# FFN down panels: low weight parts from an adding transfer instead of VectorE

## The chip, the cores and the metric

The kernel runs on one core of a Trainium2 chip. The metric is the device time of one execution in microseconds (us). The engines are named as the profile names them: PE is TensorE's matrix multiply and PEld its weight load, DVE is VectorE, ACT is ScalarE, POOL is GpSimd, and SP is SyncE, which here only issues transfers.

## What is computed

Two sequences of 256 tokens with 1024 features pass through a trunk of two layers. Each layer is a half-step gated feed-forward (FFN), a token mixer (a state-space mixer in the first layer, gated delta-net in the second), and a second FFN, each behind an RMS norm. Everything is float32. The change lies in the four FFNs:

```python
def swiglu(x, w_gu, w_down):
    gate, up = jnp.split(x @ w_gu, 2, axis=-1)
    return (jax.nn.silu(gate) * up) @ w_down

x = x + 0.5 * swiglu(rmsnorm(x, ffn1_norm[i]), ffn1_w_gu[i], ffn1_w_down[i])
```

`w_down` is 2816 by 1024. The 512 tokens are the columns of every tile, features lie on the 128 partitions.

## The kernel before, in words

To keep float32 accuracy at the matrix engine's rounded type (`fp32r`), every matrix is carried as a high part h (the value rounded to `fp32r`) and a low part l (the value less h). One product of a 128x128 weight block with a 128x512 tile is three matmuls, h·a, h·b and l·a, where a and b are the activations' two parts (lines 215, 216 and 217, in `multiply`).

The weights' parts are made in `halves`, a generator. Its inner generator `loads` walks over panels. A panel of `w_down` is one block of 128 output features, 22 weight blocks deep, so an FFN has 8 panels. SP loads up to 8 blocks into a raw tile `wr` (line 189; 512 KB for 8 blocks, 384 KB for 6; three buffers). Then, for each chunk of up to 4 blocks, ACT copies the raw values to the high tile `wh`, which rounds them (line 195; three buffers), and DVE subtracts `wh` from the raw values into the low tile `wl` (line 196; three buffers). A panel's 22 blocks are thus five chunks of 4 and one of 2. The wrapper `feed` traces one chunk ahead of the one in use.

`multiply` takes chunks from the feed and issues three matmuls per block into one PSUM tile named `pd`: 12 matmuls for a chunk of 4, 6 for a chunk of 2. All 22 blocks of a panel add up in the same `pd`. A buffer of `wh` is free again after the last line-216 matmul of its chunk, one of `wl` after the last line-217 matmul. With three buffers each, the parts of a chunk can be made while the two chunks before it are multiplied.

`ffn` first makes the hidden activations (gate and up products, tiles `p`, `pg`, `pu`). The down stage follows: a feed over the 8 panels, the first two of them cut into pieces of 8, 8 and 6 blocks and taken in turn, since the last hidden tiles come late, and then panels 2 to 7 one after the other. After each panel DVE adds the half step to the residual (line 343). Then, for the next stage, ACT and DVE split the new residual tile (lines 99 and 100), ACT squares it (line 106) and POOL adds the squares up (lines 108 and 110).

Instructions are placed on the engines' queues by the framework's planner in the order of a simulated timeline, with semaphores between engines. Each engine then works through its own queue in order; a waiting instruction holds up those behind it. POOL issues no transfer in the kernel before: all go through SP.

Of the kernel before, what the change touches and what calls it, by code (L numbers as in the profile page):

```python
# [13 lines left out]
F32 = mybir.dt.float32  # L14
F32R = mybir.dt.float32r
AF = mybir.ActivationFunctionType
ALU = mybir.AluOpType
# [20 lines left out]
class Trunk:  # L38
# [131 lines left out]
            parts.append(self.split(u[:], self.par[:, g + t:g + t + 1], self.xnp, "xn", f"xn{t}"))  # L170
        return parts

    def halves(self, panels, between=None):


        nc = self.nc
        def loads():
            for src in panels:
                for k1 in range(0, src.shape[1], 8):
                    m = min(8, src.shape[1] - k1)  # L180
                    raw = self.wr.tile([P, m, P], F32, tag="w", name="wr")
                    if between and src is panels[0]:

                        nc.sync.dma_start(raw[:, 0:4], src[:, 0:4, :])
                        between(0)
                        nc.sync.dma_start(raw[:, 4:8], src[:, 4:8, :])
                        between(1)
                    else:
                        nc.sync.dma_start(raw[:], src[:, k1:k1 + m, :])
                    for k0 in range(0, m, 4):  # L190
                        n = min(4, m - k0)
                        h = self.wh.tile([P, n, P], F32R, tag="w", name="wh")
                        l = self.wl.tile([P, n, P], F32R, tag="w", name="wl")
                        r = raw[:, k0:k0 + n, :]
                        nc.scalar.activation(h[:], r, AF.Copy)  # L195
                        nc.vector.tensor_tensor(l[:], r, h[:].bitcast(F32), op=ALU.subtract)  # L196
                        yield h, l, n
        def feed(ahead):
            while ahead is not None:
                now, ahead = ahead, next(g, None)  # L200
                yield now

        g = loads()
        return feed(next(g))

# [40 lines left out]
    def ffn(self, x, g, wgu, wd, load=None):  # L246
# [3 lines left out]
        nc, tc = self.nc, self.tc  # L250
        feed = self.halves([wgu[j, :, s] for j in range(NP) for s in range(2)], load)
# [3 lines left out]
        with tc.tile_pool(name="hid", bufs=10, reuse_waits="tile") as hp:  # L255
            hid = []
            with tc.tile_pool(name="form", bufs=6, reuse_waits="tile") as fp, \
                    tc.tile_pool(name="quad", bufs=3, reuse_waits="tile") as qp, \
                    tc.tile_pool(name="pgu", bufs=5, space=bass.MemoryType.PSUM, reuse_waits="tile") as pp:
                for j in range(NP):  # L260
# [9 lines left out]
                    a = self.t("t")  # L270
                    b = self.t("v")
# [4 lines left out]
                    h = hp.tile([P, 2, NT], F32R, name=f"h{j}", tag="p", bufs=NP)  # L276
# [10 lines left out]
                for q in range((NF - NP) // 2):  # L287
# [3 lines left out]
                    for n in range(7):  # L291
# [10 lines left out]
                        if n == 0:  # L302
                            a = sb("a", "t")
# [10 lines left out]
                        elif n == 4:  # L314
                            b = sb("b", "v")
# [11 lines left out]
            with tc.tile_pool(name="hhi", bufs=len(held), reuse_waits="tile") as hh:  # L327
                for v in held:
                    h, l = (pool.tile([P, 2, 2, 256], F32R, name="hh", tag="h") for pool in (hh, hp))
                    act(h[:], v[:], AF.Copy)  # L330
                    tt(l[:], v[:], f32(h[:]), op=ALU.subtract)
                    hid += [(h[:, :, e, :], l[:, :, e, :]) for e in range(2)]

                cut = (0, 8, 16, NF)
                feed = self.halves([wd[m][:, a:b, :] for a, b in zip(cut, cut[1:]) for m in range(2)] + [wd[m] for m in range(2, 8)])
                first = [self.multiply(feed, hid, "pd") for _ in range(2)]
                for a, b in zip(cut, cut[1:3]):
                    for f in first:
                        for _ in range(a, b):
                            next(f)  # L340
                for m in range(8):
                    p = self.run(first[m] if m < 2 else self.multiply(feed, hid, "pd"))
                    stt(x[m][:], p[:], -0.5, x[m][:], op0=ALU.mult, op1=ALU.add)
# [953 lines left out]
```

## Time and profile before

| what | us |
|---|---|
| median of two runs | 2579.3 |
| lowest and highest run | 2577.03 and 2581.57 |
| the profiled execution's own time | 2575.13 |
| its span, first to last instruction | 2573.3 |

The span is what the trace covers; about 2 us lie around it. In the rows, a line names the source line, the engine, the operation, the tile written and those read, then counts and times. `x192` is a count. "Idle before" is the time in which the engine had nothing to do just before such an instruction, and the arrow names what ended the wait. A busy matmul row is longer than the distance to the next one, since matmuls are pipelined; the distance between starts is the rate.

### The profile page before, as it was taken

The numbers are of one execution on the slowest core, as the hardware profiler recorded it, in microseconds if no ns is written. First come the engines' busy times: TensorE is split into PE (matmuls) and PEld (weight loads), VectorE is DVE, ScalarE is ACT, GpSimd is POOL, SyncE is SP. The second block draws the span as 40 slices with busy tenths as digits, with TensorE's granted clock in tenths as the row PEclk, the third lists the DMA queues.
The fourth block names the chain that finished last, engine by engine and source line by source line (L and its number), as shares of the span: only waits on it lengthen the run. The fifth ranks groups of instructions, "written<-read, shape, count | busy, mean of one in ns | idle before, by whom it ended". The sixth has DMA issues, their size and how long they took to land. (4 is left out here: it accounts for less than half of the span.)

```text
span 2573.3 us, 39462 instructions
## 1 busy us (share of the span) xinstructions
PE 2517.8 (98%) x15352; PEld 2207.1 (86%) x15352; DVE 1892.6 (74%) x2894; ACT 1227.8 (48%) x2178; POOL 361.8 (14%) x317
## 2 busy tenths in 40 slices
PE   8999999999999999999999999999999999999998
PEld 6999787777777899988999887888888988899976
DVE  6998438888874899735998537878787874799833
ACT  4445336666663544433444435445555554444521
POOL 1000004665743000000000002000100101000000
PEclk9999999999999999999999999999999999999999
DMA  4332332222222333233333343543434443333232
GB/s 154 105 108 80 90 97 71 73 84 71 81 78 91 120 108 102 72 96 112 114 107 89 94 121 109 148 114 108 123 111 120 122 126 113 120 107 107 72 97 78
DMA packets 192267, 263.32 MB, mean 102 GB/s; under 512 B 59984, under 2 KB 110416, under 8 KB 192080
## 3 DMA queue, kind: packets, MB, share of 16 engines
q1 hardware_dynamic: 192080, 260.81, 33.8%
q8 instruction: 120, 1.97, 0.3%
q14 instruction: 67, 0.55, 0.1%
HBM read 240.32 MB, written 20.45 MB: 101 GB/s over the span
## 5 line engine op out<-in xcount | busy, mean ns | idle before, releaser
L196 DVE TENSOR_TENSOR wl<-wr,wh 128x512 fp32r<-128x512 f32 (+1 forms) x525 | 380.7, 728 | 416.0 <-ACT wh L195 405.6
L195 ACT ACTIVATE wh<-wr 128x512 fp32r<-128x512 f32 (+1 forms) x525 | 319.5, 611 | 636.9 <-PE pd L216 321.7
L395 ACT ACTIVATE qh<-wq 128x1024 fp32r<-128x1024 f32 x144 | 153.0, 1062 | 183.2 <-PE p L300 143.6
L216 PE MATMUL pd<-hh,wh 128*128 128x512 f32 x576 | 228.9, 397 | 0.0
L217 PE MATMUL pd<-hh,wl 128*128 128x512 f32 x576 | 226.7, 395 | 1.3 <-DVE wl L196 1.3
L215 PE MATMUL pd<-hh,wh 128*128 128x512 f32 x576 | 226.6, 395 | 0.3
L395 ACT ACTIVATE qh<-s 128x1024 fp32r<-128x1024 f32 x108 | 114.8, 1063 | 179.6 <-PE p L300 171.8
L396 DVE TENSOR_TENSOR ql<-wq,qh 128x1024 fp32r<-128x1024 f32 x144 | 175.7, 1220 | 10.8 <-ACT qh L395 10.7
L396 DVE TENSOR_TENSOR ql<-s,qh 128x1024 fp32r<-128x1024 f32 x108 | 131.8, 1221 | 30.0 <-ACT qh L395 30.0
L108 POOL COPY acc<-sq 128x512 f32<-128x512 f32 x8 | 5.4, 680 | 1027.6 <-issue 999.4
L215 PEld LDWEIGHTS pd<-hh,wh 128*128 128x128 f32 x576 | 108.1, 188 | 29.2 <-ACT wh L195 2.0
L217 PEld LDWEIGHTS pd<-hh,wl 128*128 128x128 f32 x576 | 108.1, 188 | 28.5 <-DVE wl L196 3.0
L216 PEld LDWEIGHTS pd<-hh,wh 128*128 128x128 f32 x576 | 108.1, 188 | 25.5
L110 POOL TENSOR_TENSOR acc<-acc,sq 128x512 f32<-128x512 f32 x57 | 76.7, 1346 | 349.3 <-ACT sq L106 345.1
L215 PE MATMUL pz<-xn,wh 128*128 128x512 f32 x248 | 101.1, 408 | 2.9 <-ACT wh L195 2.9
L217 PE MATMUL pz<-xn,wl 128*128 128x512 f32 x248 | 101.0, 407 | 2.7 <-DVE wl L196 2.5
L216 PE MATMUL pz<-xn,wh 128*128 128x512 f32 x248 | 99.1, 400 | 0.9 <-DVE xn L100 0.8
L301 PE MATMUL p<-f1h,ql 128*128 128x256 f32 x288 | 82.3, 286 | 1.9 <-DVE ql L396 1.9
L300 PE MATMUL p<-f1l,qh 128*128 128x256 f32 x288 | 82.3, 286 | 0.0
L299 PE MATMUL p<-f1h,qh 128*128 128x256 f32 x288 | 82.2, 285 | 0.0
L299 PE MATMUL p<-f2h,qh 128*128 128x256 f32 x288 | 81.6, 283 | 0.0
L301 PE MATMUL p<-f2h,ql 128*128 128x256 f32 x288 | 81.5, 283 | 0.0
(491 smaller groups left out, 7911.6 us busy)
## 6 DMA issues: line engine op xcount, KB each, us to landing
wq<-in_f_gu SPq DMA_DIRECT2D x144, 512.0 KB
wr<-in_f_wd SPq DMA_DIRECT2D x64, 512.0 KB
wr<-in_ssd_w SPq DMA_DIRECT2D x48, 512.0 KB
wr<-in_gdn_w SPq DMA_DIRECT2D x48, 512.0 KB
wr<-in_f_gu SPq DMA_DIRECT2D x31, 512.0 KB
wr<-in_f_wd SPq DMA_DIRECT2D x32, 384.0 KB
wr<-in_ssd_out SPq DMA_DIRECT2D x12, 512.0 KB
wr<-in_gdn_out SPq DMA_DIRECT2D x11, 512.0 KB
```

The source lines that it names most:

```text
L108: nc.gpsimd.tensor_copy(acc[:], sq[:])
L110: nc.gpsimd.tensor_tensor(acc[:], acc[:], sq[:], op=ALU.add)
L195: nc.scalar.activation(h[:], r, AF.Copy)
L196: nc.vector.tensor_tensor(l[:], r, h[:].bitcast(F32), op=ALU.subtract)
L215: mm(p[:], h[:, q, :], a[:], start=k == 0, stop=False)
L216: mm(p[:], h[:, q, :], b[:], start=False, stop=False)
L217: mm(p[:], l[:, q, :], a[:], start=False, stop=k == K - 1)
L299: mm(p[:, e], h[:, e, k, :], fh[:, k, :], start=(e, k) == (0, 0), stop=False)
L300: mm(p[:, e], h[:, e, k, :], fl[:, k, :], start=False, stop=False)
L301: mm(p[:, e], l[:, e, k, :], fh[:, k, :], start=False, stop=(e, k) == (1, 3))
L395: nc.scalar.activation(h[:], v, AF.Copy)
L396: tt(l[:], v, h[:].bitcast(F32), op=ALU.subtract)
```

## The change

`halves` gets a flag `lean`, which only the down stage sets. With it, the low part is formed in two steps: ACT copies `wh` with scale -1 into `wl`, and a transfer issued by POOL reads the same weights from memory a second time and adds them to `wl` in place. The raw tile is still loaded by SP, and only ACT reads it. All other users of `halves` keep the subtract on DVE.

```diff
-    def halves(self, panels, between=None):
+    def halves(self, panels, between=None, lean=False):
...
                         nc.scalar.activation(h[:], r, AF.Copy)
-                        nc.vector.tensor_tensor(l[:], r, h[:].bitcast(F32), op=ALU.subtract)
+                        if lean:
+                            nc.scalar.activation(l[:], h[:].bitcast(F32), AF.Copy, scale=-1.0)
+                            nc.gpsimd.dma_start(l[:], src[:, k1 + k0:k1 + k0 + n, :], accum_op=ALU.add)
+                        else:
+                            nc.vector.tensor_tensor(l[:], r, h[:].bitcast(F32), op=ALU.subtract)
                         yield h, l, n
...
-                feed = self.halves([wd[m][:, a:b, :] for a, b in zip(cut, cut[1:]) for m in range(2)] + [wd[m] for m in range(2, 8)])
+                feed = self.halves([wd[m][:, a:b, :] for a, b in zip(cut, cut[1:]) for m in range(2)] + [wd[m] for m in range(2, 8)], lean=True)
```

## Rows read from the trace of the kernel before

**Rows 1.** The page: span and busy time of each engine.

```profile
span 2573.3 us, 39462 instructions
PE 2517.8 (98%) x15352; PEld 2207.1 (86%) x15352; DVE 1892.6 (74%) x2894; ACT 1227.8 (48%) x2178; POOL 361.8 (14%) x317
```

**Rows 2.** Four down stages: us; PE, PEld, DVE, ACT, POOL busy; clock, DMA share, GB/s.

```profile
262.00:374.00 112.00, 111.59 (x478) 89.17 (x477) 42.59 (x64) 35.82 (x59) 8.41 (x7) 1.00 0.32 96
1072.00:1184.00 112.00, 111.61 (x484) 89.50 (x483) 48.53 (x68) 37.90 (x61) 8.39 (x7) 1.00 0.29 86
1434.00:1546.00 112.00, 112.00 (x485) 90.23 (x484) 42.17 (x64) 35.41 (x59) 9.64 (x10) 1.00 0.42 125
2446.00:2558.00 112.00, 111.69 (x481) 89.74 (x480) 35.54 (x55) 29.69 (x49) 8.34 (x7) 1.00 0.28 82
```

**Rows 3.** Waits in the first down stage: who for whom; us, times, longest.

```profile
ACT wh L195 <- PE pd L216: 74.1, 44, 2.4
DVE wl L196 <- ACT wh L195: 63.7, 34, 2.6
...
PE pd L217 <- DVE wl L196: 0.3, 1, 0.3
```

**Rows 4.** Timeline of the matmuls, 300 to 307 us: start, length, first matmuls of chunks.

```profile
300.71 0.39 PE L215 MATMUL pd<-hh,wh 128*128 128x512 f32 x1
...
303.51 0.39 PE L215 MATMUL pd<-hh,wh 128*128 128x512 f32 x1
...
306.31 0.39 PE L215 MATMUL pd<-hh,wh 128*128 128x512 f32 x1
```

**Rows 5.** Timeline of PEld: the weight load of that last chunk's first low part.

```profile
306.55 0.19 PEld L217 LDWEIGHTS pd<-hh,wl 128*128 128x128 f32 x1
```

**Rows 6.** Timeline of ACT, 296 to 316 us.

```profile
298.84 0.73 ACT L99 ACTIVATE xn<-x,par 128x512 fp32r<-128x512 f32 x1 [0.32 <-DVE x L343]
299.47 0.62 ACT L106 ACTIVATE sq<-x 128x512 f32<-128x512 f32 x1
300.74 0.63 ACT L195 ACTIVATE wh<-wr 128x512 fp32r<-128x512 f32 x1 [0.66 <-PE pd L216]
...
306.28 0.42 ACT L195 ACTIVATE wh<-wr 128x256 fp32r<-128x256 f32 x1 [2.12 <-PE pd L216]
```

**Rows 7.** Timeline of DVE, 296 to 316 us: low parts of 4 and of 2 blocks.

```profile
301.41 0.69 DVE L196 TENSOR_TENSOR wl<-wr,wh 128x512 fp32r<-128x512 f32 x1 [1.06 <-ACT wh L195]
...
306.73 0.42 DVE L196 TENSOR_TENSOR wl<-wr,wh 128x256 fp32r<-128x256 f32 x1 [1.85 <-ACT wh L195]
```

**Rows 8.** Timeline of POOL, 262 to 400 us: sums per panel, the longest operation.

```profile
300.23 1.30 POOL L110 TENSOR_TENSOR acc<-acc,sq 128x512 f32<-128x512 f32 x1 [14.10 <-ACT sq L106]
315.63 1.30 POOL L110 TENSOR_TENSOR acc<-acc,sq 128x512 f32<-128x512 f32 x1 [14.10 <-ACT sq L106]
...
386.52 2.94 POOL L169 TENSOR_TENSOR t<-x,rstd 128x512 f32<-128x512 f32 x1 [6.40 <-DVE xn L100]
```

**Rows 9.** The chain of waits, 2085 to 2120 us: two 256 KB loads, release to landing.

```profile
2090.18 2.45 DMA ob<-opark
...
2109.86 3.22 DMA ob<-opark
```

**Rows 10.** The tile ob: SP's issue of such a load, ns min/median/max.

```profile
L992 SPq DMA_DIRECT2D ob<-opark x12: 319/319/447, 2082.9 to 2114.6; - x12
```

**Rows 11.** Groups of POOL: a small and a large one; busy us, mean ns.

```profile
L169 POOL TENSOR_TENSOR t<-x,rstd 128x512 f32<-128x512 f32 x4 | 8.4, 2112 | 12.8 <-DVE xn L100 12.8
...
L127 POOL TENSOR_TENSOR sr<-sv,mhalf 128x4 f32<-128x4 f32 x8 | 8.2, 1022 | 87.0 <-DVE sv L126 87.0
```

**Rows 12.** Transfers, 262 to 374 us: packets, MB, share of 16 engines.

```profile
q1 hardware_dynamic: 3168, 10.62, 31.9%
```

**Rows 13.** The chain of waits, 1794 to 1804 us: the slowest 256 KB transfer read.

```profile
1796.55 5.79 DMA CU<-dtt
```

**Rows 14.** A gapped stretch of the second mixer, columns as in rows 2.

```profile
1700.00:1760.00 60.00, 52.99 (x375) 48.21 (x374) 43.21 (x122) 28.36 (x80) 7.22 (x9) 0.97 0.31 83
```

## The prediction

> **What bounds the kernel now.** The page comes first. Matmuls are busy 98% of the span, DVE 74%, ACT 48%, POOL 14% [rows 1]. Only work taken off PE, or PE's idle time, can shorten the kernel. So I look at the stretches that the change touches. Inside the four down stages PE is busy at least 111.59 of 112 us at the full granted clock, while DVE stands at 36 to 49 us and ACT at 30 to 38 [rows 2]. The waits say the same from the other side: PE waited 0.3 us in all for a low part, once, while DVE waited 63.7 us for ACT, and ACT 74.1 us for PE to give a buffer back [rows 3]. So neither DVE nor ACT is late: both are held by the three buffers, and the parts lie ready long before their use. The reader should take from this that the change removes work from an engine that PE does not wait for. What decides is whether its replacement still fits into the time that three buffers give.
>
> That time is read from the timelines. Chunks of 4 blocks start at 300.71, 303.51 and 306.31, so a chunk lasts 2.80 us [rows 4], and a chunk of 2 by half the matmuls 1.40. A panel is five and a half such, 15.40, which is the distance of POOL's sums [rows 8]. The chunk at 306.31 uses the buffers of the one that ended at 300.71. Its high part was started at 300.74 for 0.63 us [rows 6], its low part at 301.41 for 0.69 [rows 7], so it was ready at 302.10. It was wanted at 306.55 [rows 5]: 4.45 us to spare.
>
> **The change part by part.**
>
> *Removed from DVE.* 4 FFNs with 8 panels give 160 subtracts of 0.69 and 32 of 0.42 us [rows 7]: 124 us of DVE, next to nothing of it waited for by PE. If all idle PE time of rows 2 came back, that is 1.1 us over the four stretches. I take 0 and keep -1.
>
> *Added to ACT.* 192 negations of the shape of line 195, 0.63 or 0.42 us [rows 6]: 114 us. Per panel ACT then does 5 x 1.26, 0.84 and the 1.35 of lines 99 and 106: 8.5 of 15.4 us. It stays off the bound as a rate. The negation waits for `wl`'s buffer, which comes one matmul after `wh`'s; queued behind it are the next line 195, 99 and 106, which are due later anyway. It costs its own length in the latency below.
>
> *Moved.* The raw tile is released by ACT instead of DVE, 0.7 us earlier; SP's next load waits for that release, with three tiles of two chunks ahead. Worth 0; it makes the next load coincide with the adding transfer of the same chunk. POOL's one sum of 1.30 us per panel [rows 8] shares its queue with six issues; a sum queued behind them is not due before the next norm, but a chunk's issue behind a sum can be late by up to 1.30.
>
> *Added: the transfer.* No row shows a transfer issued by POOL or one that adds, so I bound it. Call D the time from the end of the negation to the landing.
> - Issue: at the least what SP takes, 0.32 [rows 10]; POOL's small two-input operation takes 1.02, a large one 2.11 on the mean [rows 11]. I take 1.02, because an issue touches little data.
> - Movement and landing: a plain 256 KB load took 2.45 to 3.22 us with SP's issue of 0.32 inside [rows 9, 10], and the slowest 256 KB transfer read took 5.79 [rows 13]. I take 3.22 less 0.32, 2.90, because every adding transfer runs beside the panels' loads.
> - The add: the destination must be read too. At worst this costs as much engine time as moving the bytes once. In the first stretch 10.62 MB took 31.9% of 16 engines over 112 us [rows 12], that is 35.7 us, so 0.262 MB takes 0.88. At best it overlaps and costs 0. I take 0.88.
>
> D = 1.02 + 2.90 + 0.88 = 4.80 us. The ends are 2.45 (issue as SP's, free add) and 1.02 + 5.47 + 0.88 = 7.37; with an issue of 2.11 as well, 8.46.
>
> The 256 KB row can be weighed against a rule. The Trainium skill ("DMA: Bandwidth & Descriptors", Anatomy of one DMA) gives a POOL-issued transfer about 2.0 us plus its bytes at 436 GB/s, so 2.6 by estimate, and in Latency and other measured facts about 1 us to the first byte; as an estimate D would be 3.6, which is the hidden case below. Rows 9 agree for SP's transfers; no run here shows POOL's. The rule that speaks against the change is in "Collectives: The Full Stack" (The bandwidth ceiling): an adding transfer reads two sources over one queue and moves half as fast. That would make the estimate 4.2, and the cost +28 us.
>
> **The sum.** After a chunk ends, its buffer's next low part is negated 1.33 us later (300.71 to 301.37 for the high part, 0.04 hand-over as in rows 6 and 7, 0.63 for the negation: 302.04), with 0.04 to reach POOL: 1.37. PE wants the part 0.24 after a chunk's start [rows 4, 5]. So the next chunk in that buffer can't start before 1.13 + D after the last one ended. Each buffer serves two chunks per panel. The buffers that hold two chunks of 4 come round in 2 x 2.80 + 2 x (1.13 + D) = 7.86 + 2D. A panel needs 15.40, so the break-even is D = 3.77, and beyond it a panel lengthens by 2 us for each us of D. With 32 panels:
>
> cost = 64 x (D - 3.77) = 64 x 1.03 = +66 us.
>
> The profiled execution took 2575.1, which is 4.2 below the median of the runs; on it the sum gives **2641 us**, +2.6%. A 60 us stretch with PE busy 88% was granted 0.97 of the clock [rows 14]; the lap above leaves PE 88% busy as well, which would add at most 3% of the 5.6 us of matmul in a lap, 0.17 x 32 = 5 us. I leave that in the range.
>
> **The rivals.**
> - *Hidden.* D stays below 3.77: POOL issues in about a third of a microsecond, or landing is the 2.45 of the quiet row and the add is free (2.45 + 0.70 = 3.15 with POOL's issue). Then the panel's own 15.40 covers it, and time stays at 2574 to 2576. For it: 4.45 us of slack in a full chunk. Against it: the short chunk takes 1.40 of that from two chunks per panel (3.05 is left), and the pair of half panels at a stage's start has two short chunks close together. This is the side "not slower"; it decides at D = 3.77 for no cost, and at D = 4.57 for less than 51 us.
> - *The transfer is much slower*, because adding bytes move slower than copied ones, or the queues fill: raw loads already use 0.28 to 0.42 of the transfer engines [rows 2], and the added ones read as many bytes again from memory and from `wl`. At 7.37 the cost is 64 x 3.60 = +230: 2805 us. Against it: the quiet rows of the same size stay at or under 3.22.
> - *POOL's queue is the bound.* Six issues per panel of 2.11 and a sum of 1.30 take 14.0 us, under 15.4; only from 2.35 us per issue would the queue itself set the pace. At the 2.94 of POOL's longest operation [rows 8] per issue, six and a sum take 18.9, and 32 panels lose 3.5 each: +114, 2689 us. It would show as POOL going from issue to issue without a wait.
> - *Faster.* The planner orders all queues by its own timeline, and with other orders elsewhere the time may move; DVE's 124 us lie where PE does not wait. To gain 2% PE would have to lose idle time of 51 us, and the whole span holds 2573.3 - 2517.8 = 55.5 [rows 1], 1.1 of it in these stretches. 3%.
>
> **How the numbers follow.** I give the exposed landing (D from 3.8 to 6.2) 0.60, hidden 0.20, slower transfer or POOL-bound 0.17, another order that gains 0.03. About 2%, 51 us, is what a measurement of this kernel can tell from no change; that is D = 4.57. Of the 0.60 I put 0.48 above that and 0.12 below; with the 0.17 slower gets 0.65, same 0.20 + 0.12 = 0.32, faster 0.03. The likeliest case alone runs from 2577 to 2731 (D = 6.2). The range takes in the hidden case and most of the slow one: 2573 to 2780, which is D = 6.97.
>
> **What would show it.** Right: in the down stages PE waits for `wl` at line 217, two or three times a panel, and the panel's distance at POOL's sums goes from 15.40 to about 17.5; DVE's busy time falls by about 124 us and ACT's rises by 114; bytes read rise by 46 MB (192 chunks, 4 x 11.5). The wait of ACT for `pd` stays, that of DVE for `wh` is gone there. The waits should fall on the first two chunks after a short one. Wrong: if PE stays at 111.6 of 112, D is below 3.77 and the transfer is cheaper than rows 9 and 11 say; if all chunks are late alike, D is far above 5 or POOL's issues are the bound; if the lost time lies outside the four stretches, the planner's order has changed and the lap is not the cause.

## The result and the profile after

The changed kernel took 2686.63 us (median of two runs, 2685.92 to 2687.34) against 2579.3: slower, ratio 1.0436 with a 95% interval of 1.042 to 1.0453. Its span is 2685.5 us, 112.2 longer. The page of the kernel after, its parts on engines and queues (compare [rows 1]):

```profile
span 2685.5 us, 39810 instructions
PE 2540.4 (95%) x15352; PEld 2203.6 (82%) x15352; DVE 1774.6 (66%) x2702; ACT 1331.9 (50%) x2370; POOL 531.2 (20%) x509
...
q1 hardware_dynamic: 192080, 260.81, 32.2%
q0 software_dynamic: 27648, 46.15, 11.5%
...
L198 POOL DMA_DIRECT2D wl<-in_f_wd x192 | 168.0, 884 | 1267.3 <-ACT wl L197 649.3
...
L221 PE MATMUL pd<-hh,wl 128*128 128x512 f32 x576 | 236.8, 413 | 64.7 <-DMA wl<-in_f_wd 64.1
```

DVE lost 118 us of work and ACT gained 104, near the 124 and 114 forecast, and 46.15 MB come on a new queue. The last line is the price: the matmul of the low part, which had waited next to never [rows 3], now sits idle 64.7 us before its groups on `hh` alone, and what it waits for is the adding transfer. The line numbers have moved by 4: 217 is 221 here.

Panels are best measured by DVE's residual update, one per panel. Its timeline in the second down stage of the kernel after:

```profile
1133.85 0.69 DVE L347 SCALAR_TENSOR_TENSOR x<-pd,x 128x512 f32<-128x512 f32 x1 [3.87 <-PE pd L221]
1152.71 0.69 DVE L347 SCALAR_TENSOR_TENSOR x<-pd,x 128x512 f32<-128x512 f32 x1 [16.40 <-PE pd L221]
1170.64 0.69 DVE L347 SCALAR_TENSOR_TENSOR x<-pd,x 128x512 f32<-128x512 f32 x1 [15.48 <-PE pd L221]
1188.46 0.69 DVE L347 SCALAR_TENSOR_TENSOR x<-pd,x 128x512 f32<-128x512 f32 x1 [15.36 <-PE pd L221]
```

Between these the distance is 17.8 to 18.9 us where it was 15.40 [rows 8]. Taken over all panels by the same rows, the six later panels of a stage lost 17.6, 19.0, 26.7 and 16.9 us in the four stages, 80.2 in all; the stretch from the previous stage's end to the end of the second panel lost 5.1, 8.9, 8.9 and 9.1, 32.0 in all. Together that is the 112.2. The second kind of stretch also holds the mixers and the gate and up stages; that its loss arises at the starts of the down stages is shown by the experiment on them below.

How a late part arises is seen in one round of the buffers. The timeline of POOL in the kernel after, then the weight loads that waited for a transfer:

```profile
1149.97 0.86 POOL L198 DMA_DIRECT2D wl<-in_f_wd  x1 [2.37 <-ACT wl L197]
1152.77 0.89 POOL L198 DMA_DIRECT2D wl<-in_f_wd  x1 [1.94 <-ACT wl L197]
1154.17 0.87 POOL L198 DMA_DIRECT2D wl<-in_f_wd  x1 [0.51 <-ACT wl L197]
1155.05 1.31 POOL L110 TENSOR_TENSOR acc<-acc,sq 128x512 f32<-128x512 f32 x1
1158.24 0.88 POOL L198 DMA_DIRECT2D wl<-in_f_wd  x1 [1.88 <-DMA wl<-in_f_wd]
1162.22 0.86 POOL L198 DMA_DIRECT2D wl<-in_f_wd  x1 [3.10 <-ACT wl L197]
1164.58 0.88 POOL L198 DMA_DIRECT2D wl<-in_f_wd  x1 [1.50 <-ACT wl L197]
1167.89 0.87 POOL L198 DMA_DIRECT2D wl<-in_f_wd  x1 [2.42 <-ACT wl L197]
```

```profile
1154.14 0.19 PEld L221 LDWEIGHTS pd<-h,wl 128*128 128x128 f32 x1 [1.44 <-DMA wl<-in_f_wd]
1158.10 0.19 PEld L221 LDWEIGHTS pd<-hh,wl 128*128 128x128 f32 x1 [1.33 <-DMA wl<-in_f_wd]
1163.79 0.19 PEld L221 LDWEIGHTS pd<-hh,wl 128*128 128x128 f32 x1 [0.25 <-DMA wl<-in_f_wd]
1166.60 0.19 PEld L221 LDWEIGHTS pd<-hh,wl 128*128 128x128 f32 x1 [0.18 <-DMA wl<-in_f_wd]
```

Take the buffer of the chunk whose low part was loaded at 1154.14. From the stalled matmul to the chunk's end is 2.33 us. The timeline of ACT shows the two copies that follow:

```profile
1156.54 0.63 ACT L195 ACTIVATE wh<-wr 128x512 fp32r<-128x512 f32 x1 [1.65 <-PE pd L220]
1157.21 0.63 ACT L197 ACTIVATE wl<-wh 128x512 fp32r<-128x512 f32 x1
```

The negation ends at 1157.84, 1.37 after the chunk. POOL begins the issue at 1158.24, 0.40 later, and that transfer lands 5.5 us after the issue began; PE goes on at 1163.79. These add up: 2.33 + 1.37 + 0.40 + 5.5 + 0.05 = 9.65. The same buffer's next turn is issued at 1167.89 and lands 4.2 later, 8.37 in all. One lap of this buffer is 18.02 us, and that is the panel. POOL itself is mostly idle: between issues it waits 0.5 to 3 us.

Landings of the 256 KB transfers fall in two classes. The view of line 198 over a window that holds a single issue gives 4.1 to 4.3 us for those at 1149.97, 1162.22 and 1167.89, and 5.2 to 5.5 for those at 1152.77, 1154.17 and 1158.24. (The one at 1164.58 carries the 128 KB of a short chunk; it took 4.2.) Another adding transfer in flight does not tell the classes apart: the quick one at 1162.22 was issued while that of 1158.24 was in flight. What does is SP's load of the next raw tile, moved by the same 16 engines. The timeline of SP has an issue 1.0 us before two of the slow ones, the second of which has no other adding transfer issued within 3.9 us:

```profile
1151.73 0.33 SPq L189 DMA_DIRECT2D wr<-in_f_wd  x1
...
1157.20 0.33 SPq L189 DMA_DIRECT2D wr<-in_f_wd  x1
```

Counted over the trace, 97 of the 160 transfers of 256 KB had a transfer issued by SP in the 3 us before their own issue; they landed in 5.5 us on the median (4.1 to 8.6). The other 63 landed in 4.2 (4.0 to 4.9). Among those with no other adding transfer issued within 3 us, the medians are 5.4 (19 transfers) and 4.2 (9). The kernel's last panel has no load left beside it: its transfers at 2652.40 and 2653.80 follow each other by 1.40 us, as those at 1152.77 and 1154.17 do, and land in 4.0 and 4.9 us. No run moved SP's load alone, so this is read from the trace. The answers for 1158.24, 2652.40 and 2653.80, and the one over all 192:

```profile
DMA to landing us min/median/max: 5.5/5.5/5.5
...
DMA to landing us min/median/max: 4.0/4.0/4.0
...
DMA to landing us min/median/max: 4.9/4.9/4.9
...
DMA to landing us min/median/max: 3.2/4.8/8.6
```

The third stage lost most, 26.7 us in the later panels. Busy time by stretch, kernel after, columns as in [rows 2]:

```profile
1134.00:1207.00 73.00, 63.31 (x263) 48.15 (x262) 5.65 (x9) 32.92 (x57) 25.57 (x28) 1.00 0.77 156
1512.00:1592.00 80.00, 67.33 (x264) 51.76 (x263) 5.65 (x9) 33.00 (x57) 25.57 (x29) 0.94 0.74 155
```

The same work took 80 us there instead of 73. PE stood idle 12.7 us instead of 9.7, and the granted clock was 0.94 of the 2.4 GHz level instead of 1.00. By PE's busy and idle time, 4.0 of the 7 us are slower matmuls and 3.0 longer waits. The residual tiles are parked in memory in this stage as well; what that adds to the waits was not separated.

### The profile page after: what moved, and what is told of

It reads as the page before. It is cut to its first block, busy times and chain, and to the rows that moved or that the text cites. A ratio compares the mean times of both kernels' runs of the same rounds, so it can differ in the third digit from the quotient of the medians.

```text
span 2685.5 us, 39810 instructions
## 1 busy us (share of the span) xinstructions
PE 2540.4 (95%) x15352; PEld 2203.6 (82%) x15352; DVE 1774.6 (66%) x2702; ACT 1331.9 (50%) x2370; POOL 531.2 (20%) x509
## 3 DMA queue, kind: packets, MB, share of 16 engines
q0 software_dynamic: 27648, 46.15, 11.5%
## 5 line engine op out<-in xcount | busy, mean ns | idle before, releaser
L198 POOL DMA_DIRECT2D wl<-in_f_wd x192 | 168.0, 884 | 1267.3 <-ACT wl L197 649.3
L200 DVE TENSOR_TENSOR wl<-wr,wh 128x512 fp32r<-128x512 f32 (+1 forms) x333 | 259.7, 782 | 191.5 <-ACT wh L195 184.5
L221 PE MATMUL pd<-hh,wl 128*128 128x512 f32 x576 | 236.8, 413 | 64.7 <-DMA wl<-in_f_wd 64.1
L220 PE MATMUL pd<-hh,wh 128*128 128x512 f32 x576 | 231.6, 402 | 0.0
L219 PE MATMUL pd<-hh,wh 128*128 128x512 f32 x576 | 230.8, 401 | 0.0
L347 DVE SCALAR_TENSOR_TENSOR x<-pd,x 128x512 f32<-128x512 f32 x24 | 16.6, 692 | 321.3 <-PE pd L221 321.3
L197 ACT ACTIVATE wl<-wh 128x512 fp32r<-128x512 f32 x192 | 113.2, 593 | 5.3
L347 DVE SCALAR_TENSOR_TENSOR xg<-pd,xg 128x512 f32<-128x512 f32 x8 | 5.5, 692 | 132.0 <-PE pd L221 132.0
```

What stands on the lines that cost most here:

```text
L197: nc.scalar.activation(l[:], h[:].bitcast(F32), AF.Copy, scale=-1.0)
L198: nc.gpsimd.dma_start(l[:], src[:, k1 + k0:k1 + k0 + n, :], accum_op=ALU.add)
L219: mm(p[:], h[:, q, :], a[:], start=k == 0, stop=False)
L220: mm(p[:], h[:, q, :], b[:], start=False, stop=False)
L221: mm(p[:], l[:, q, :], a[:], start=False, stop=k == K - 1)
```

## The experiments

**Traffic without a reader.** DVE's subtract is back; negation and adding transfer go into spare tiles.

```diff
                         nc.scalar.activation(h[:], r, AF.Copy)
                         if lean:
-                            nc.scalar.activation(l[:], h[:].bitcast(F32), AF.Copy, scale=-1.0)
-                            nc.gpsimd.dma_start(l[:], ..., accum_op=ALU.add)
-                        else:
-                            nc.vector.tensor_tensor(l[:], r, h[:].bitcast(F32), op=ALU.subtract)
+                            s = lean.tile([P, n, P], F32R, tag="s", name="ws")
+                            nc.scalar.activation(s[:], h[:].bitcast(F32), AF.Copy, scale=-1.0)
+                            nc.gpsimd.dma_start(s[:], ..., accum_op=ALU.add)
+                        nc.vector.tensor_tensor(l[:], r, h[:].bitcast(F32), op=ALU.subtract)
```

> The subtract on VectorE is back and forms the low part; the negation and the adding transfer are kept, but go into four spare tiles that no matmul reads. If the landing is what PE waits for (buffer lap), nothing waits for these transfers: 2579 to 2590 us, PE gap-free in the down stages, panels 15.4 apart, although the transfer engines carry the same extra 46 MB. If the extra traffic itself, or POOL's queue, slows the weights (rate), it stays at 2640 us or above.

2600.22 us, beside 2576.47 for the kernel before on the same chip: 10 more than expected. All later panels were 15.40 us apart; the excess of 25 us lay before the second panel's end of each stage (6.2, 6.6, 7.8 and 4.3). The timeline of ACT in this run, first stage:

```profile
245.89 7.68 ACT L335 ACTIVATE hh<-hq 128x1024 fp32r<-128x1024 f32 x8
253.47 1.66 ACT L198 ACTIVATE ws<-wh 128x512 fp32r<-128x512 f32 x3
255.55 0.61 ACT L195 ACTIVATE wh<-wr 128x512 fp32r<-128x512 f32 x1
```

The first negation into a spare tile stands behind the eight copies of the hidden tiles, and the next high part behind the negation: that part starts at 255.55, where in the kernel before it started at 242.74, ahead of those copies. PE then waited 5.6 us for DVE's low part. Why the planner placed the negation there was not shown; memory for the spare tiles that comes free late is likely. That is a fault of this experiment, so it was run again with the spare tiles only from the third panel on:

> As e1, but negation and adding transfer into the spare tiles only from the third panel on, 144 instead of 192 transfers, since e1's whole excess lay before its first panel ended, where the first spare tile held up ScalarE's queue. Lap theory: extra traffic costs nothing by itself, 2575 to 2582 us, panels 15.40 apart. If the traffic slows the start of a stage too, 2590 us or more.

2574.69 us, beside a median of 2573.96 for the kernel before. Busy time by stretch of this run:

```profile
288.00:360.00 72.00, 72.00 (x310) 57.91 (x309) 25.17 (x37) 38.36 (x66) 29.31 (x32) 1.00 0.91 189
1134.00:1184.00 50.00, 50.00 (x216) 40.20 (x215) 18.36 (x26) 26.78 (x47) 22.59 (x24) 1.00 0.91 187
```

PE has no gap at all, although the transfer engines are busy 0.91 of the time and move 187 to 189 GB/s, more than after the change (155 to 156 above). Neither the extra bytes nor the negations nor POOL's issues cost anything where nobody waits for them. The rate as such is ruled out; the wait for the landing is left.

**A plain transfer.** The transfer overwrites the low part instead of adding, so the low part is the raw weight.

```diff
-                            nc.gpsimd.dma_start(l[:], ..., accum_op=ALU.add)
+                            nc.gpsimd.dma_start(l[:], ...)
```

> The transfer issued by POOL overwrites the low part instead of adding to it (the low part is then the raw weight, so the output differs); issue, waits and bytes loaded stay. If reading the destination costs about what was forecast, 0.88 us per landing, landing falls from 4.2 alone to about 3.3 us, a panel shortens by 1.8 us and the time is about 2630 us. If the add is free, the landing stays near 4.2 us and the time at 2687. If the add is most of the landing (2 us or more), the panels return to 15.4 and the time to about 2580.

2636.7 us, 7 off the first case. The timeline of POOL in this run, two issues of 256 KB with none of SP's in the 3 us before, and the landings of all 192:

```profile
1148.53 0.53 POOL L198 DMA_DIRECT2D wl<-in_f_wd  x1 [3.21 <-ACT wl L197]
...
1154.12 0.53 POOL L198 DMA_DIRECT2D wl<-in_f_wd  x1 [2.69 <-ACT wl L197]
```

```profile
DMA to landing us min/median/max: 2.3/3.2/6.2
```

An issue takes 0.53 instead of 0.87 us, and these two land in 2.9 us each instead of 4.1 to 4.3. Adding thus costs about 1.3 us per transfer, a quarter of it POOL's longer issue, and 50 of the 107 us of the kernel. Behind a transfer of SP, plain ones landed in 3.9 us on the median, adding ones in 5.5. A transfer issued by POOL that adds nothing would still be late: later panels of the second stage took 16.0 to 17.8 us.

**Negating the raw tile.** The negation no longer reads the high part.

```diff
                         if lean:
-                            nc.scalar.activation(l[:], h[:].bitcast(F32), AF.Copy, scale=-1.0)
+                            nc.scalar.activation(l[:], r, AF.Copy, scale=-1.0)
                             nc.gpsimd.dma_start(l[:], ..., accum_op=ALU.add)
+                            nc.scalar.activation(h[:], r, AF.Copy)
```

> ScalarE negates and rounds the raw tile into the low part before it makes the high part, so the negation no longer comes after the high part: it ends 0.80 instead of 1.33 us after the chunk that frees the buffer. Lap theory: two such per lap and panel, 1.06 us x 32 = 34 us less, about 2653 us. If the transfers' rate or POOL's queue sets the pace, no change, 2687.

2664.57 us: 22 less instead of 34, and not where it was expected. The stages' starts gave back 24 us, the later panels nothing: in the second stage most took 18.2 to 18.6, where they had taken 17.8 to 18.5. The timeline of ACT in this run shows that the copy still came first:

```profile
1149.74 0.63 ACT L198 ACTIVATE wh<-wr 128x512 fp32r<-128x512 f32 x1 [3.62 <-issue]
1150.28 0.61 ACT L196 ACTIVATE wl<-wr 128x512 fp32r<-128x512 f32 x1
```

The negation follows 0.54 after the copy's start instead of 0.67, so the edit saved 0.13 us of latency, not 0.53. The order in the source was not the order in the queue, so the later panels of this run do not test the lap. What it changed at the stages' starts is told below.

**Four low buffers.** The same, with `wl` in four buffers.

```diff
-        self.wl = pool("wlo", 3)
+        self.wl = pool("wlo", 4)
```

> As e3, with four instead of three buffers of low parts. A low part can then be begun three chunks ahead: 8.4 us of cover (7.0 beside a short chunk) against 1.3 + 0.4 + 4.2 to 5.9 us from the freed buffer to the landing. Lap theory: hidden nearly everywhere, 2580 to 2595 us. If the transfer engines, 77% busy in a down stage after the change, are the bound, shorter panels fill them and it stays above 2630.

2585.7 us, as the lap predicts. All transfers, all negations and all of POOL's issues are still there, and 101 of the 107 us are gone. The tile `pd` in this run, what ended PE's and PEld's idle time:

```profile
  DMA wl<-in_f_wd: 20.4, 39
```

In the kernel after the same answer has 203.8 us, 134 times. Which of the two edits does it was asked with the buffer alone, on the changed kernel:

> The change as it is, with four buffers of low parts and still three of high parts. The negation reads the high part, which waits for its own buffer, so the low part can't be begun earlier: lap theory says 2680 to 2690 us, no gain, and e4's gain came from both edits together. If the low buffers alone were what was short, it falls to 2590 like e4.

2699.97 us: no gain, 13 more than the kernel after, on one run and at a granted clock of 0.982 against 0.989. Why it lost these 13 was not followed up. The forecast was 2680 to 2690. The negation reads `wh`, whose three buffers still set the pace, so a fourth low buffer can't be begun earlier. Both edits are needed.

**The stages' starts.** The first two panels, taken in turn, have DVE's subtract again.

```diff
-            for src in panels:
+            for at, src in enumerate(panels):
...
-                        if lean:
+                        if lean and at >= lean:
...
-                feed = self.halves(..., lean=True)
+                feed = self.halves(..., lean=6)
```

> The first two panels (taken in turn, in half panels) have their subtract on VectorE again, panels 2 to 7 keep the change. The stages' starts up to the end of the second panel were 32 us longer in all four together: 2655 us if that share is the two panels' own late landings, 2687 if it comes from elsewhere (the planner's order of the gate and up stage).

2652.68 us. The second panel's end is as before again (within 0.6 us in three stages, 2.2 later in the fourth), so nearly all of the 32 us was lost by these two panels themselves. The trace of the kernel after shows how. The timeline of ACT at the start of the second stage, PE's longest wait there, and its longest ahead of the short chunks in the run that negates the raw tile:

```profile
1096.03 0.63 ACT L195 ACTIVATE wh<-wr 128x512 fp32r<-128x512 f32 x1 [0.75 <-PE pd L220]
1098.83 0.63 ACT L195 ACTIVATE wh<-wr 128x512 fp32r<-128x512 f32 x1 [2.17 <-PE pd L220]
1101.63 0.63 ACT L195 ACTIVATE wh<-wr 128x512 fp32r<-128x512 f32 x1 [2.17 <-PE pd L220]
1102.17 1.14 ACT L197 ACTIVATE wl<-wh 128x512 fp32r<-128x512 f32 x2
...
1107.73 0.79 PE L221 MATMUL pd<-hh,wl 128*128 128x512 f32 x1 [4.97 <-DMA wl<-in_f_wd]
...
1105.21 0.50 PE L222 MATMUL pd<-hh,wl 128*128 128x512 f32 x1 [0.55 <-DMA wl<-in_f_wd]
```

The chunk copied at 1096.03 is negated only at 1102.17: two further copies, which wait for PE to give buffers back, stand ahead of the negations in ACT's queue. Each stage's start has one such wait, 4.75, 4.97, 5.04 and 5.12 us, 19.9 of the 32. In the run that negates the raw tile, copies and negations take turns from the start, and the longest waits ahead of the short chunks are 0.5 to 0.7 us; most of the 24 us that it gave back lies here. Beside the short chunks of the pair PE waited 1.4 to 1.7 us per stage.

**Smaller transfers.** Each chunk's transfer in two halves, the kernel otherwise as after.

```diff
-                            nc.gpsimd.dma_start(l[:], src[:, k1 + k0:k1 + k0 + n, :], accum_op=ALU.add)
+                            for q in range(0, n, 2):
+                                nc.gpsimd.dma_start(l[:, q:q + 2, :], src[:, k1 + k0 + q:k1 + k0 + q + 2, :], accum_op=ALU.add)
```

> The change as it is, with each chunk's adding transfer split into two of 2 blocks (128 KB). If a matmul waits only for the half it reads, the first half is due as before and lands like the 128 KB ones (median 4.1 us), the second half 1.4 us later: lap theory with D shorter by about 1 us for the first half, 0.5 us or less for the second, 2610 to 2660 us. If POOL's issues or the number of transfers set the pace (12 instead of 6 issues per panel), it is slower than 2687.

2701.8 us, 15 more than the kernel after: the forecast was wrong. A pair of issues, and matmuls on the chunk's low part, in the timelines of POOL and PE:

```profile
1160.74 1.77 POOL L199 DMA_DIRECT2D wl<-in_f_wd  x2 [3.78 <-ACT wl L197]
```

```profile
1163.88 0.47 PE L222 MATMUL pd<-h,wl 128*128 128x512 f32 x1
1164.65 0.40 PE L222 MATMUL pd<-h,wl 128*128 128x512 f32 x1
1166.85 0.50 PE L222 MATMUL pd<-h,wl 128*128 128x512 f32 x1 [1.34 <-DMA wl<-in_f_wd]
```

Two blocks go on as soon as the first half is there (its landing took 3.0 us from 1160.74), and the third block stalls: the matmuls do wait by halves, but the second half, issued behind the first, lands 6.1 us after the pair began. SP issued the next raw load at 1162.50, beside it. Over this trace the second halves landed in 5.5 us on the median where SP issued a transfer between 3.5 us before and 1.5 us after them, and in 3.9 elsewhere, counted from their own issue. Halving the bytes bought less time than the second issue and such a load beside it cost.

**Does any form beat the kernel before?** The best form, timed several times, with its control (the kernel before with `wl` in four buffers), and the form for the first two panels alone (`at < 6`), where DVE still has the hidden tiles' low parts to make:

> The kernel of e4 again, timed in rounds. Lap theory: with the landing covered, taking 124 us of VectorE's work away gains nothing, since no matmul waited for it; the rest of e4's excess over the kernel before (9 us) is late landings beside short chunks: ratio 1.002 to 1.006. A ratio below 1 would mean that VectorE's work did hold the kernel up.

> The kernel before with four buffers of low parts and nothing else, the control for e10: the parts already lie ready, so 2570 to 2580 us, no difference.

> e4's form (raw negation, four low buffers) for the first two panels alone, the subtract on VectorE for the others. In e4 three of four stage starts were 0.9 to 1.3 us shorter than before, the fourth 2.9 longer, while later panels lost 11 us. So 2574 to 2580 us, within 0.2% of the kernel before; the theory that a free VectorE helps the stage's start would show as 3 us or more gained.

The best form has the ratio 1.0042 (1.0027 to 1.0057) to the kernel before: 0.4% slower, with most of the landing covered. In the profiled execution its later panels took 11.7 us more in all than 15.40 each, which covers the excess of 9.9. The control has 1.0003 (0.9993 to 1.0013) and the first two panels alone 0.9994 (0.9984 to 1.0003): no difference that can be measured. No version beats the kernel before.

## Why the prediction was right, step by step

The forecast was 2641 us, the measured time 2686.6: the direction and the mechanism came out, the size was 46 us short.

- *What bounds.* Right. PE did not wait for DVE, so taking 124 us (118 measured) from DVE gained nothing: with most of the landing covered the time is 1.0042 of before, not below, and what is left is accounted for by late parts.
- *The lap of three buffers.* Right as a mechanism: panels lengthen, the first two chunks after a short one wait most (1.44 and 1.33 us against 0.25 and 0.18), and a fourth low buffer that can really be begun earlier removes it. A constant was off. I let the weight load run 0.24 us into the chunk, as in [rows 5]. A stalled part lets matmul and load start together, 0.47 into the chunk, so the lap is about 7.5 + 2D, and the break-even about 3.95 instead of 3.77.
- *D, alone.* Forecast 4.80 and measured 0.41 + 4.2 = 4.6, by errors that cancel, which is luck: the issue took 0.87, not 1.02; the hand-over from ACT to POOL 0.41, not the 0.04 of ACT to DVE; the add 1.3, not 0.88; the plain transfer lands 2.9 after its issue began, not 1.02 + 2.90.
- *D, beside a load.* This is the first term that was mis-sized, and a reason why 112 us came of a forecast 66. I took 3.22 as the landing for all transfers, since all were to run beside the panels' loads, and priced the meeting of the next load with the adding transfer at 0. Behind a transfer of SP the adding ones land 5.5 us after their issue on the median, so D is 5.9; elsewhere 4.6. One of the two turns in the lap followed above is of the slow kind, 9.65 and 8.37 us, which give 18.0 instead of the forecast 17.5. With D of 4.6 in both, the lap would be 16.7.
- *The pair at the start.* Forecast like all others, 8 x 2.06 = 16 us; it lost 32. The sum let every negation follow its copy at once. At a stage's start two more copies stood ahead of it in ACT's queue, one wait of about 5 us per stage, 19.9 in all. The two short chunks close together, which the rival on the hidden case named, are the smaller part: 1.4 to 1.7 us per stage.
- *The other rivals.* Hidden: no. Even the plain transfer, whose single landing makes a D of 3.3, lost 60 us; behind SP's transfers it makes 4.3. POOL's queue as the bound: no, it waits between issues and six of 0.87 take a third of a panel. A much slower add: no, at 1.3. Transfer engines too busy: not as a bound by themselves, as the traffic without a reader shows, but the loads beside an adding transfer delay its landing.

The Trainium skill ("DMA: Bandwidth & Descriptors", Anatomy of one DMA) gave an estimate of 2.6 us for a plain 256 KB transfer; single plain ones landed in 2.9 here, issue included. "Collectives: The Full Stack" (The bandwidth ceiling) was the rule against the change, stated there for rings of several cores: two source reads, half the speed, 0.6 us more by estimate. The direction agrees; the measured add is twice that, and 0.34 of it lies on POOL, of which the rule says nothing.

## What to carry to other kernels

Moving work off an engine that nobody waits for gained nothing here, and its replacement is judged by latency: add up copy, hand-over, issue and landing, and hold them against the time that the buffers give, at the shortest chunks. Take the landing as it is beside the loads that share the engines, and read from the queue what stands ahead of the first step. A transfer in this chain of three buffers needed a buffer more, and the whole chain had to be free to start earlier: a fourth low buffer alone gave nothing, and with a negation that no longer read the high part it gave back 101 of 107 us. To learn whether bytes or waiting cost the time, keep the traffic and take away its reader.

## What the runs showed of the hardware

An adding transfer of 256 KB issued by POOL took 0.87 us of POOL's queue and landed 4.2 us after the issue began on the median, against 0.53 and 2.9 for a plain one; with a transfer issued by SP in the 3 us before, 5.5 and 3.9. POOL began an issue 0.40 to 0.41 us after ACT's negation ended, ten times what DVE needed after ACT [rows 6, 7]. Transfer engines busy 0.91 of the time at 187 to 189 GB/s delayed no matmul whose parts came from DVE.
